# A hybrid decoder layer on one core: 24 of 32 activation tiles turned by VectorE and stored block by block, and three smaller edits in TensorE's and ScalarE's order

## The chip, the core and the metric

The kernel runs on one core of a Trainium2 chip. The metric is the device time of one execution in microseconds (us), given as the median of several runs. PE is TensorE, PEld its weight loads, DVE is VectorE, ACT is ScalarE, POOL is GpSimd, SP is SyncE, which here only issues DMAs; SPq is its queue. A line such as L825 is a line of the kernel before.

## What is computed

One layer of a decoder trunk over 2048 tokens of width 1024, all in float32. Cut to what matters:

```python
xn   = rms_norm(x, mix_norm_w)                       # 2048 x 1024
proj = xn @ w_in                                     # six groups of 512 columns: q, f, v, g, lru_x, lru_gate
mixed = concat(hgrn2(q, f, v, g), rglru(lru_x, lru_gate))   # chunkwise recurrences over the tokens
h    = x + mixed @ w_out
hn   = rms_norm(h, ffn_norm_w)                       # h * (mean(h^2) + eps)^-0.5 * ffn_norm_w
gate, up = split(hn @ w_gate_up)                     # 2 x 2816 columns
h    = h + (silu(gate) * up) @ w_down
out  = rms_norm(h, final_norm_w)
```

## The kernel before

**Stages.** The tokens go through in two halves of 1024, and each half in two pieces of 512 or eight tiles of 128 tokens. The order of the program is: half 0's mixers and output projection, half 1's mixers and output projection (the first loop `for half in range(2)`), then for half 0 the gate/up products (`ffn_up`) and the down products (`down_quads`), then the same for half 1. Every large product is three float32r matmuls of rounded parts (high by high, low by high, high by low), so one 128x512 block costs three passes per 128 rows of depth. The output projection, gate/up and down products take seven block products in place of eight (names p1 to p7; the banks `quad_a`, `quad_e`, `quad_f`, `quad_g` hold them in gate/up).

**What `h_steps` does (lines 1377 to 1404).** After the output projection, h lies in DRAM by tokens. The gate/up products need hn with features on the partitions. So for each of the 8 tiles of a half, `scale` loads the two 512-wide pages of the tile (n = 0 and 1, names `hs`), takes the sum of squares on ACT, the factor on DVE and POOL, and multiplies on DVE. `turn` then turns each page with `transposed` (lines 245 to 249): four 128x128 transposes on PE (L248, tiles `tp_hs`) into a PSUM bank of the tag `aux`, a copy to SBUF by ACT (L1398, tiles `hths` of the tag `late`, five buffers), and one store on SP's queue (L1399) into the DRAM tensor `hn`, whose rows are features. That makes 32 pages, 16 in each half.

**Where these steps stand.** Half 0's steps are the list `later` that is emptied in the next pass of the loop, one entry behind each of the eight `tok_mm` of half 1's first product (lines 1183 to 1188, tiles `pv`, 24 matmuls each). Half 1's steps run in half 0's `ffn_up`: the list has 14 empty entries and then 14 for each tile, one taken behind each of the seven products of a quad, so that one tile is scaled and turned in every two quads. Half 0's hn is read again in half 1's output projection, half 1's in half 0's `down_quads`; both are far behind the stores.

**Who sets the order.** The program is written in the order above, but a scheduler with its own simulated clock sets the order of instructions on each engine; each engine then runs its list in order and waits at semaphores. `tc.issue_after(ins)` puts what the block creates behind `ins`, for instructions of `ins`'s own engine. The buffers of a tag are given out in turn (`late` 5, `aux` 4 banks, `mm` 4 banks, the split weights `w` 9).

**The other places that the change touches.** `diagonals` and `over_rows` (lines 595 to 606) and `row_spread` (608 to 615) spread 512 row factors over all partitions: a diagonal matrix of the factors is multiplied by a matrix of ones, four float32 matmuls of 128x128. They are used three times besides the first piece of half 0: for the second piece of half 0 (L614) and for both pieces of half 1 (L605). In `ffn_up` the seven products of the first quad of a half are made in the order p1, p5, p6, p7, p2, p3, p4; p3 adds to the bank of p5 (`quad_e`), so its first matmul can't start before ACT has copied that bank out (L870). At the end of the last `down_quads`, `square` and `finish` normalise the last tiles: for each, the sum is squared on ACT (L980), the root taken on ACT (L993), its reciprocal on DVE (L994), then the rows are scaled on both engines and stored. The chains `behind("act", ...)` and `behind("dve", ...)` keep these in order. `root_table` (L998 to L1001) is to load ACT's table for the root early: it calls a bare table load inside `issue_after` of a matmul, with no data that it reads.

Of the kernel before, what the change touches and what calls it, by code (L numbers as in the profile page):

```python
# [9 lines left out]
F32R = mybir.dt.float32r  # L10
AF = mybir.ActivationFunctionType
ALU = mybir.AluOpType

P = 128
# [9 lines left out]
CW = 512  # L24
NC = T // CW
TPC = CW // P
NTT = T // P
SUB = 32
# [9 lines left out]
def hybrid_layer(ctx: ExitStack, tc: tile.TileContext, x, x_t, norm_w, cols, w_in, gate_w, w_out, w_gu, w_down, out):  # L38
    nc = tc.nc
    const = ctx.enter_context(tc.tile_pool(name="const", bufs=1))  # L40
# [5 lines left out]
    def f(t):  # L46
        return t.bitcast(F32)
# [17 lines left out]
    def late(nm):  # L65
        return sb.tile([P, CW], F32, tag="late", name=nm, bufs=5)
# [4 lines left out]
    def aux(nm):  # L71
        return psp.tile([P, CW], F32, tag="aux", name=nm)
# [27 lines left out]
    v = nc.vector  # L100
    ones = const.tile([P, 1], F32, name="ones")
    nc.gpsimd.memset(ones, 1.0)
    tinies = const.tile([P, 17, 4], F32, name="tinies")
    n4 = [0]

# [139 lines left out]
    def transposed(tt, n, src, nm):  # L245
        ps = aux("tp_%s_%d" % (nm, n))
        for j in range(4):
            nc.tensor.transpose(out=ps[:, j * P : (j + 1) * P], in_=src[:, j * P : (j + 1) * P], identity=ident)  # L248
        return ps.rearrange("p (k t) -> p k t", t=P)
# [343 lines left out]
        return xw  # L593

    def diagonals(c, rs, nm):
        dg = late("dg" + nm)
        for tt in range(TPC):
            v.tensor_scalar(out=dg[:, tt * P : (tt + 1) * P], in0=ident, scalar1=rs[:, tt : tt + 1], scalar2=None, op0=ALU.mult)
        return dg

    def over_rows(dg, nm):
        pbc = aux("tpb" + nm)
        for tt in range(TPC):
            ts = slice(tt * P, (tt + 1) * P)
            nc.tensor.matmul(pbc[:, ts], lhsT=ones.broadcast_to([P, P]), rhs=dg[:, ts], start=True, stop=True)  # L605
        return pbc

    def row_spread(c, rs, nm="x0"):
        nm = f"{nm}_{c}"
        pbc, dg = aux("tpb" + nm), late("dg" + nm)  # L610
        for tt in range(TPC):
            ts = slice(tt * P, (tt + 1) * P)
            v.tensor_scalar(out=dg[:, ts], in0=ident, scalar1=rs[:, tt : tt + 1], scalar2=None, op0=ALU.mult)
            nc.tensor.matmul(pbc[:, ts], lhsT=ones.broadcast_to([P, P]), rhs=dg[:, ts], start=True, stop=True)  # L614
        return pbc
# [170 lines left out]
    class Sums:  # L786
# [8 lines left out]
        def make(self, i):  # L795
# [21 lines left out]
            split([w[:, s, :] for s in range(2)], x)  # L817
            self.op[name] = w

    def product(ps, w, b, first):  # L820
        for k in range(4):
            ks = slice(k * P, (k + 1) * P)
            hi, lo = b[0][:, k, :], b[1][:, k, :]
            for n, (s, x) in enumerate(((0, hi), (1, hi), (0, lo))):
                ins = nc.tensor.matmul(  # L825
                    ps, lhsT=w[:, s, ks], rhs=x, start=first and k + n == 0, stop=k == 3 and n == 2, skip_group_check=not first
                )
        return ins.ins


# [15 lines left out]
    def ffn_up(half, bops, between=()):  # L846
        between = list(between)
        q0 = half * 2 * NPAIR
        for q in range(q0, q0 + 2 * NPAIR):
# [7 lines left out]
            for i, name in enumerate(ORDER):  # L857
                if q == q0 and i not in s.done:
                    s.make(i)
                if q == q0 and name == "p2":  # L860
                    with tc.issue_after(last):
                        last = product(dst[name], s.op.pop(name), bops[name], False)
                else:
                    last = product(dst[name], s.op.pop(name), bops[name], i < 4)
                if name == "p1":
                    e1 = page("e1" + nm)
                    nc.scalar.copy(out=e1, in_=b1)
# [129 lines left out]

    def root_table(matmul):  # L998
        with tc.issue_after(matmul.ins):
            ins = nc.scalar.preload_act_table(AF.Sqrt)  # L1000
        tail["act"] = ins.ins  # L1001

    def behind(eng, make):
# [72 lines left out]
    def down_quads(half, groups, hp, extra):  # L1076
# [18 lines left out]
        for s, (gr, i) in enumerate(seq):  # L1095
# [10 lines left out]
            for tt in range(TPC):  # L1106
                tsl = slice(tt * P, (tt + 1) * P)
                ps = banks[tt]
                for q in range(gr.n):
                    ahi, alo = (z[:, tsl] for z in a[q])  # L1110
                    whi, wlo = (w[z][:, q, :] for z in range(2))
                    for n, (x, y) in enumerate(((ahi, whi), (ahi, wlo), (alo, whi))):
                        ins = nc.tensor.matmul(  # L1113
                            ps, lhsT=x, rhs=y, start=first and q + n == 0, stop=q == gr.n - 1 and n == 2, skip_group_check=not first
                        )
                if half and end and name == "p5" and tt == 0:
                    root_table(ins)
                g = c * TPC + tt
                if half and end and name in ("p3", "p4"):
# [30 lines left out]
    for half in range(2):  # L1150
# [226 lines left out]
        def h_steps(g, half=half, ffn_row=ffn_row):  # L1377
            ps = []
            nm = f"hs{half}_{g}"

            def scale():
                if not ffn_row:
                    ffn_row.append(wvec(1, f"wffn{half}"))
                for n in range(2):
                    p = page(f"{nm}_{n}")
                    nc.sync.dma_start(out=p, in_=h_d[half][g][n])
                    ps.append(p)
                rs = rstd_of(ps, nm)
                for n in range(2):
                    v.scalar_tensor_tensor(  # L1390
                        out=ps[n], in0=ps[n], scalar=rs, in1=ffn_row[0][:, n * CW : (n + 1) * CW], op0=MUL, op1=MUL
                    )

            def turn():
                for n in range(2):
                    pt = transposed(g, n, ps[n], nm)
                    q = late(f"ht{nm}_{n}")
                    nc.scalar.copy(out=q.rearrange("p (k t) -> p k t", t=P), in_=pt)  # L1398
                    nc.sync.dma_start(  # L1399
                        out=hn_d[half][n][:, :, g * P : (g + 1) * P].rearrange("k p t -> p k t"),  # L1400
                        in_=q.rearrange("p (k t) -> p k t", t=P),
                    )

            return scale, turn

# [122 lines left out]
```

## Time and profile before

| | us |
|---|---|
| median of three runs | 2062.3 (2061.43 to 2062.76) |
| the profiled execution: device time | 2061.29 |
| the profiled execution: span of the trace | 2059.6 |

The profile is one execution. Its span goes from the first to the last instruction or transfer; 1.69 us of the device time lie around it. "busy" is the time in which an engine had an instruction in work. A wait is given with the engine, line and tile that ended it. A timeline row gives start, length, engine, line, operation, tiles, shapes and a count of merged instructions; the length of a merged PE row includes the tail of its last matmul, which overlaps the next row, so the pace is read from starts. The chain of work that ended last gives the start and length of each link.

### The profile page before, as it was taken

To read this page: it belongs to the slowest core of one execution; us is meant where nothing else is said; L and a number is where in the kernel's file an instruction comes from. 1 tells how busy PE (TensorE), PEld (TensorE's weight loads), DVE (VectorE), ACT (ScalarE), POOL (GpSimd) and SP (SyncE) were. 2 spreads that over 40 slices of the span, in tenths; PEclk is the share of its full clock that TensorE was granted. 3 is DMA by queue.
4 is the path that set the end of the run, shared out by engine and by line. 5 is a ranking of instruction groups with operands and counts; after the bars stand their busy time and mean duration, and the time that the engine had idled before them with its cause. 6 is when DMAs were issued, how large, how long until landed. Compare 5 with 4: busy or idle time off the path is not lost.

```text
span 2059.6 us, 26494 instructions
## 1 busy us (share of the span) xinstructions
PE 2050.5 (100%) x9532; PEld 1702.7 (83%) x9532; DVE 1557.8 (76%) x2581; ACT 1023.0 (50%) x1700; POOL 196.8 (10%) x339
## 2 busy tenths in 40 slices
PE   9999999999999999999999999999999999999998
PEld 8888888888888888888888888888888888888887
DVE  7878779836887699877777778879776676667766
ACT  8677765456776545343343344346433333344434
POOL 1001100000000000322222210001110010010000
PEclk9999999999999999999999999999999999999999
DMA  7234115831111365655555588665432232268642
GB/s 287 93 104 138 56 42 211 290 123 42 42 42 42 106 223 173 211 183 183 185 184 179 179 307 301 236 213 189 138 133 91 84 133 97 85 250 289 226 156 103
DMA packets 160228, 326.84 MB, mean 159 GB/s; under 512 B 14432, under 2 KB 31072, under 8 KB 160096
## 3 DMA queue, kind: packets, MB, share of 16 engines
q1 hardware_dynamic: 140448, 261.40, 37.4%
q0 software_dynamic: 19360, 63.45, 8.5%
q8 instruction: 75, 1.23, 0.3%
q14 instruction: 57, 0.47, 0.1%
q10 hardware_dynamic: 288, 0.29, 0.0%
HBM read 242.77 MB, written 82.31 MB: 158 GB/s over the span
## 4 chain that ended last, share of the span: by engine, by line
PE 95%; ACT 2%; DVE 1%; DMA 1%; issue 0%; POOL 0%; SPq 0%; DVEq 0%; ACTq 0%
PE quad_e L825 12%; PE quad_g L825 12%; PE quad_a L825 12%; PE pda L1113 11%; PE pdb L1113 8%; PE quad_f L825 6%; PE pox L1357 4%; PE poyp L1357 3%; PE pa L260 2%; PE pa L261 2%; PE pa L262 2%; PE pb L262 2%; PE pb L261 2%; PE pb L260 2%; PE pv L638 2%; PE pg L273 1%
## 5 line engine op out<-in xcount | busy, mean ns | idle before, releaser
L825 PE MATMUL quad_a<-act_a,wgu_a 128*128 128x512 f32 x528 | 132.3, 390 | 0.0
L825 PE MATMUL quad_e<-act_c,wgu_c 128*128 128x512 f32 x528 | 128.4, 389 | 0.5 <-ACT e L870 0.5
L825 PE MATMUL quad_e<-act_e,wgu_e 128*128 128x512 f32 x528 | 128.7, 389 | 0.0
L825 PE MATMUL quad_g<-act_g,wgu_g 128*128 128x512 f32 x528 | 127.6, 389 | 0.0
L825 PE MATMUL quad_f<-act_f,wgu_f 128*128 128x512 f32 x528 | 127.5, 389 | 0.0
L825 PE MATMUL quad_a<-act_b,wgu_b 128*128 128x512 f32 x528 | 127.1, 389 | 0.0
L825 PE MATMUL quad_g<-act_d,wgu_d 128*128 128x512 f32 x528 | 126.8, 389 | 0.0
L825 PEld LDWEIGHTS quad_e<-act_c,wgu_c 128*128 128x128 f32 x528 | 99.1, 188 | 21.4 <-ACT e L870 0.9
L825 PEld LDWEIGHTS quad_a<-act_b,wgu_b 128*128 128x128 f32 x528 | 99.1, 188 | 20.7
L825 PEld LDWEIGHTS quad_g<-act_g,wgu_g 128*128 128x128 f32 x528 | 99.1, 188 | 20.6
L825 PEld LDWEIGHTS quad_e<-act_e,wgu_e 128*128 128x128 f32 x528 | 99.1, 188 | 20.6
L825 PEld LDWEIGHTS quad_g<-act_d,wgu_d 128*128 128x128 f32 x528 | 99.1, 188 | 20.6
L825 PEld LDWEIGHTS quad_f<-act_f,wgu_f 128*128 128x128 f32 x528 | 99.1, 188 | 20.5
L825 PEld LDWEIGHTS quad_a<-act_a,wgu_a 128*128 128x128 f32 x528 | 98.5, 188 | 19.9
L681 DVE TENSOR_TENSOR u<-u,quad_g 128x512 f32<-128x512 f32 x88 | 60.2, 684 | 64.0 <-PE quad_g L825 64.0
L260 PE MATMUL pa<-xn,whi_in 128*128 128x512 f32 x256 | 101.5, 397 | 0.1
L262 PE MATMUL pb<-xn,whi_in 128*128 128x512 f32 x256 | 100.4, 392 | 0.0
L261 PE MATMUL pa<-xn,wlo_in 128*128 128x512 f32 x256 | 100.4, 392 | 0.0
L261 PE MATMUL pb<-xn,wlo_in 128*128 128x512 f32 x256 | 100.4, 392 | 0.0
L262 PE MATMUL pa<-xn,whi_in 128*128 128x512 f32 x256 | 100.4, 392 | 0.0
L260 PE MATMUL pb<-xn,whi_in 128*128 128x512 f32 x256 | 100.1, 391 | 0.0
L292 ACT ACT_TABLE_LOAD x69 | 88.5, 1283 | 2.4 <-PEq L1517 1.2
(373 smaller groups left out, 4971.5 us busy)
## 6 DMA issues: line engine op xcount, KB each, us to landing
raw<-in_w_gu SPq DMA_DIRECT2D x88, 512.0 KB, 4.1
raw_in<-in_w_in SPq DMA_DIRECT2D x47, 512.0 KB, 3.6
ao_p<-as POOLq DMA_DIRECT2D x88, 256.0 KB, 2.7
b<-hn SPq DMA_DIRECT2D x48, 256.0 KB, 3.9
wds<-in_w_down POOLq DMA_DIRECT2D x44, 256.0 KB, 4.4
wd_p<-wds POOLq DMA_DIRECT2D x44, 256.0 KB, 2.7
x<-in_x SPq DMA_DIRECT2D x32, 256.0 KB, 5.4
res<-in_x SPq DMA_DIRECT2D x32, 256.0 KB, 6.4
```

Of the source, the lines that this page charges most:

```text
L260: nc.tensor.matmul(ps, lhsT=whi[:, ks], rhs=hi, start=(k == 0), stop=False)
L261: nc.tensor.matmul(ps, lhsT=wlo[:, ks], rhs=hi, start=False, stop=False)
L262: nc.tensor.matmul(ps, lhsT=whi[:, ks], rhs=lo, start=False, stop=(k == KT - 1))
L273: nc.tensor.matmul(ps, lhsT=hi, rhs=wlo[:, ks], start=False, stop=False)
L292: in_line(lambda: nc.scalar.preload_act_table(func))
L638: ins = nc.tensor.matmul(banks[tt], lhsT=a, rhs=w, start=(k + i == 0), stop=(k == KT - 1 and i == 2))
L681: return (e or v).tensor_tensor(out=out, in0=a, in1=b, op=op)
L825: ins = nc.tensor.matmul(ps, lhsT=w[:, s, ks], rhs=x, start=first and k + n == 0, stop=k == 3 and n == 2, skip_group_check=not first)
L1113: ins = nc.tensor.matmul(ps, lhsT=x, rhs=y, start=first and q + n == 0, stop=q == gr.n - 1 and n == 2, skip_group_check=not first)
L1357: nc.tensor.matmul(ps, lhsT=x_, rhs=y_, start=first and q + m == 0, stop=q == 3 and m == 2, skip_group_check=not first)
```

## The change

- `turn` in `h_steps`: for both pages of half 1's tiles and for page n = 0 of half 0's, 24 pages of 32, the four PE transposes and ACT's copy are replaced by one DVE instruction (`v.transpose`, on chip a STREAM_TRANSPOSE) that turns each 32x32 block of the 128x512 page in place of the whole. The blocks are put in their places by the store: four DMAs of 32 partitions x 16 blocks x 32 elements, 64 KB each in runs of 128 bytes, where one DMA of 256 KB in runs of 512 bytes stood. The eight n = 1 pages of half 0 stay as they were.
- `diagonals` and `over_rows`: the factors are split into a rounded part and a rest, two float32r diagonals of 512 columns, and two 128x512 matmuls with a rounded matrix of ones add up in one bank. `row_spread` uses them for the second piece of half 0; its first piece stays as it was. On DVE there are eight instructions of 128x128 where there were four.
- First quad of a half in `ffn_up`: p3 is to come behind the middle of p7 on PE.
- `root_table`: instead of the bare load, a root of the first tile's running sum into a column that is overwritten later; it is called behind p7's first tile and no longer behind p5's.

```diff
     def diagonals(c, rs, nm):
-        dg = late("dg" + nm)
+        dg = [sb.tile([P, CW], F32R, tag="late", name=f"dg{s}{nm}", bufs=5) for s in range(2)]
         for tt in range(TPC):
-            v.tensor_scalar(out=dg[:, tt * P : (tt + 1) * P], in0=ident, scalar1=rs[:, tt : tt + 1], scalar2=None, op0=ALU.mult)
+            ts, r = slice(tt * P, (tt + 1) * P), rs[:, tt : tt + 1]
+            v.tensor_scalar(out=dg[0][:, ts], in0=ident, scalar1=r, scalar2=None, op0=ALU.mult)
+            v.scalar_tensor_tensor(out=dg[1][:, ts], in0=ident, scalar=r, in1=f(dg[0][:, ts]), op0=ALU.mult, op1=ALU.subtract)
...
-        for tt in range(TPC):
-            ts = slice(tt * P, (tt + 1) * P)
-            nc.tensor.matmul(pbc[:, ts], lhsT=ones.broadcast_to([P, P]), rhs=dg[:, ts], start=True, stop=True)
+        for s in range(2):
+            nc.tensor.matmul(pbc, lhsT=ones_r.broadcast_to([P, P]), rhs=dg[s], start=(s == 0), stop=(s == 1))
...
+                elif q == q0 and name == "p3":
+                    with tc.issue_after(mid):
+                        last = product(dst[name], s.op.pop(name), bops[name], False)
...
+                if q == q0 and name == "p7":
+                    mid = halfway["ins"]
...
     def root_table(matmul):
         with tc.issue_after(matmul.ins):
-            ins = nc.scalar.preload_act_table(AF.Sqrt)
+            ss = sums_f[1, 0]
+            ins = nc.scalar.activation(out=ss[:, 3:4], in_=ss[:, 2:3], func=AF.Sqrt)
...
                 for n in range(2):
-                    pt = transposed(g, n, ps[n], nm)
                     q = late(f"ht{nm}_{n}")
-                    nc.scalar.copy(out=q.rearrange("p (k t) -> p k t", t=P), in_=pt)
-                    nc.sync.dma_start(
-                        out=hn_d[half][n][:, :, g * P : (g + 1) * P].rearrange("k p t -> p k t"),
-                        in_=q.rearrange("p (k t) -> p k t", t=P),
-                    )
+                    if half or n == 0:
+                        v.transpose(out=q, in_=ps[n])
+                        to = hn_d[half][n].rearrange("k (u a) t -> a (k u) t", a=SUB)
+                        for i in range(TPC):
+                            t1 = g * P + i * SUB
+                            nc.sync.dma_start(
+                                out=to[:, :, t1 : t1 + SUB],
+                                in_=q[i * SUB : (i + 1) * SUB].rearrange("p (j b) -> p j b", b=SUB),
+                            )
+                    else:
...
```

Here is how three places move. In the rows of the changed kernel the line numbers are its own (L248 is L250 there, L825 is L832, L232 is L234, L980 is L994). The numbers at the end of a name are those of buffers.

PE in half 1's first product, behind its third tile of tokens (`pv_0_2`); `tp_hs_1_0` and `tp_hs_1_1` are the turned pages of half 0's tile 1. Before:

```order
L273 MATMUL pv_0_2_3847<-wlo_in_3_3690,xn_0_01_3388 128x512
L274 MATMUL pv_0_2_3847<-whi_in_3_3689,xn_0_11_3390 128x512
L248 MATMUL tp_hs_1_0_3886<-ident,hs_1_0_3818 128x128 x4
L248 MATMUL tp_hs_1_1_3894<-ident,hs_1_1_3820 128x128 x4
L272 MATMUL pv_0_3_3902<-whi_in_0_3671,xn_0_00_3387 128x512
L273 MATMUL pv_0_3_3902<-wlo_in_0_3672,xn_0_00_3387 128x512
```

and now:

```order
L275 MATMUL pv_0_2_3856<-wlo_in_3_3701,xn_0_01_3399 128x512
L276 MATMUL pv_0_2_3856<-whi_in_3_3700,xn_0_11_3401 128x512
L250 MATMUL tp_hs_1_1_3902<-ident,hs_1_1_3831 128x128 x4
L274 MATMUL pv_0_3_3909<-whi_in_0_3682,xn_0_00_3398 128x512
L275 MATMUL pv_0_3_3909<-wlo_in_0_3683,xn_0_00_3398 128x512
```

Four of the eight transposes between two tiles of tokens are gone; in half 0's `ffn_up` all eight between two quads are.

PE in the first quad of half 0's `ffn_up`: `quad_e_0_0<-act_c` is the first matmul of p3, `quad_f` is p6, `quad_g` p7, `quad_a_0_1` the next quad's p1. Before:

```order
L825 MATMUL quad_a_0_1_7360<-act_a_0_6789,wgu_a_0_1_7233 128x512
L825 MATMUL quad_e_0_0_7216<-act_c_0_7175,wgu_c_0_0_7205 128x512
L825 MATMUL quad_f_0_0_7217<-act_f_0_6982,wgu_f_0_0_7172 128x512 x2
L825 MATMUL quad_f_0_0_7217<-act_f_0_6983,wgu_f_0_0_7172 128x512
L825 MATMUL quad_f_0_0_7217<-act_f_0_6982,wgu_f_0_0_7172 128x512 x2
```

and now:

```order
L832 MATMUL quad_a_0_1_7355<-act_a_0_6784,wgu_a_0_1_7228 128x512
L832 MATMUL quad_f_0_0_7212<-act_f_0_6977,wgu_f_0_0_7167 128x512 x2
L832 MATMUL quad_f_0_0_7212<-act_f_0_6978,wgu_f_0_0_7167 128x512
L832 MATMUL quad_f_0_0_7212<-act_f_0_6977,wgu_f_0_0_7167 128x512 x2
L832 MATMUL quad_f_0_0_7212<-act_f_0_6978,wgu_f_0_0_7167 128x512
L832 MATMUL quad_g_0_0_7213<-act_g_0_6979,wgu_g_0_0_7182 128x512 x2
L832 MATMUL quad_g_0_0_7213<-act_g_0_6980,wgu_g_0_0_7182 128x512
L832 MATMUL quad_g_0_0_7213<-act_g_0_6979,wgu_g_0_0_7182 128x512 x2
L832 MATMUL quad_g_0_0_7213<-act_g_0_6980,wgu_g_0_0_7182 128x512
L832 MATMUL quad_e_0_0_7211<-act_c_0_7170,wgu_c_0_0_7200 128x512
```

p3's first matmul has moved behind twelve matmuls of p6 and p7.

ACT in the last group of the last `down_quads`: `jf` are squares of finished rows, `aop_g` the split operand of p7. Before, the table load of `root_table` is the fourth row of ACT's whole list (L1000, behind the load of the parameters), and another one stands ahead of the first root (L993). Here nothing stands between the third square and p7's operand:

```order
L980 ACTIVATE jf_1_0_16877,sf_1_16876<-hd_1_0_15689 128x512
L980 ACTIVATE jf_2_0_16900,sf_2_16899<-hd_2_0_15691 128x512
L232 CAST aop_g_1_8_17032<-ra_g_1_8_16954 128x1024
L232 CAST aop_g_1_8_17046<-ra_g_1_8_16956 128x512
L980 ACTIVATE jf_3_0_16919,sf_3_16918<-hd_3_0_15693 128x512
```

and now:

```order
L994 ACTIVATE jf_1_0_16840,sf_1_16839<-hd_1_0_15652 128x512
L994 ACTIVATE jf_2_0_16863,sf_2_16862<-hd_2_0_15654 128x512
L1015 ACT_TABLE_LOAD
L1015 ACTIVATE sf_0_16816<-sf_0_16816 128x1
L234 CAST aop_g_1_8_16994<-ra_g_1_8_16917 128x1024
L234 CAST aop_g_1_8_17008<-ra_g_1_8_16919 128x512
```

The load at the start of ACT's list and the load ahead of the first real root are both gone; one load and a root of one column stand ahead of p7's operand.

More of the change, by code (lines that the diff above doesn't have):

```diff
@@ L102, in hybrid_layer @@
     nc.gpsimd.memset(ones, 1.0)
+    ones_r = const.tile([P, 1], F32R, name="ones_r")
+    nc.gpsimd.tensor_copy(out=ones_r, in_=ones)
     tinies = const.tile([P, 17, 4], F32, name="tinies")
@@ L609, in row_spread @@
         nm = f"{nm}_{c}"
+        if c:
+            return over_rows(diagonals(c, rs, nm), nm)
         pbc, dg = aux("tpb" + nm), late("dg" + nm)
@@ L818, in make @@
             self.op[name] = w
+    halfway = {}
     def product(ps, w, b, first):
@@ L827, in product @@
                 )
+            if k == 1:
+                halfway["ins"] = ins.ins
         return ins.ins
@@ L1115, in down_quads @@
                         )
-                if half and end and name == "p5" and tt == 0:
+                if half and end and name == "p7" and tt == 0:
                     root_table(ins)
@@ L1395, in turn @@
                 for n in range(2):
-                    pt = transposed(g, n, ps[n], nm)
                     q = late(f"ht{nm}_{n}")
-                    nc.scalar.copy(out=q.rearrange("p (k t) -> p k t", t=P), in_=pt)
-                    nc.sync.dma_start(
-                        out=hn_d[half][n][:, :, g * P : (g + 1) * P].rearrange("k p t -> p k t"),
-                        in_=q.rearrange("p (k t) -> p k t", t=P),
-                    )
+                    if half or n == 0:
[8 more added lines that the diff above has]
+                    else:
+                        pt = transposed(g, n, ps[n], nm)
+                        nc.scalar.copy(out=q.rearrange("p (k t) -> p k t", t=P), in_=pt)
+                        nc.sync.dma_start(
+                            out=hn_d[half][n][:, :, g * P : (g + 1) * P].rearrange("k p t -> p k t"),
+                            in_=q.rearrange("p (k t) -> p k t", t=P),
+                        )
             return scale, turn
```

## The prediction, made before the changed kernel was run

> **What bounds the kernel.** I read the page first: busy shares and the chain that ended last.
>
> ```profile
> span 2059.6 us, 26494 instructions
> PE 2050.5 (100%) x9532; PEld 1702.7 (83%) x9532; DVE 1557.8 (76%) x2581; ACT 1023.0 (50%) x1700; POOL 196.8 (10%) x339
> PE 95%; ACT 2%; DVE 1%; DMA 1%; issue 0%; POOL 0%; SPq 0%; DVEq 0%; ACTq 0%
> ```
>
> PE is in work for 2050.5 of 2059.6 us. The waits of PE say the same: three in the whole program, 1.5 us.
>
> ```profile
> PE warm L543 <- PEq L1517: 0.8, 1, 0.8
> PE quad_e L825 <- ACT e L870: 0.5, 1, 0.5
> PE pr L468 <- DVE v L435: 0.2, 1, 0.2
> ```
>
> So a PE instruction that goes away is time gained one for one, as long as what replaces it doesn't make PE wait; work added on DVE, SP or the DMA engines costs nothing until then. The sum below prices PE's work by pace (start to start), not by the length of a row, since neighbouring rows overlap.
>
> **Part 1: transposes of half 1's 16 pages.** The chain of waits has one link of quad_g per quad. While tiles are turned, two quads take one period, and after the last turned tile one quad.
>
> ```profile
> 920.93 2.72 PE quad_g L825 x12
> ...
> 959.91 2.72 PE quad_g L825 x12
> ...
> 1173.64 2.72 PE quad_g L825 x12
> ...
> 1192.68 2.72 PE quad_g L825 x12
> ```
>
> The period with a turned tile is 959.91 - 920.93 = 38.98 us; two quads without are 2 x (1192.68 - 1173.64) = 38.08 us, which is 168 matmuls at 2.72/12 = 0.227 us. Eight transposes cost 0.90 us, and eight tiles 8 x 0.90 = 7.2 us.
>
> **Part 2: transposes of half 0's n = 0 pages.** The timeline of PE in half 1's first product has a group of eight behind every 24 matmuls; two groups are 412.03 to 418.37 = 6.34 us apart, and 24 x 0.227 = 5.44, so again 0.90 us for eight. Four stay. What a group of four small ones costs is seen at the old row factors, in half 0's output projection:
>
> ```profile
> 412.03 1.04 PE L248 MATMUL tp_hs<-ident,hs 128*128 128x128 f32 x8
> 418.37 1.03 PE L248 MATMUL tp_hs<-ident,hs 128*128 128x128 f32 x8
> 338.52 0.61 PE L605 MATMUL tpbx<-dgx,ones 128*128 128x128 f32 x4
> 339.20 0.40 PE L1357 MATMUL pox<-wlo_o_p,mx_f 128*128 128x512 f32 x1
> ```
>
> From 338.52 to 339.20 there are four small passes and one wide matmul: 0.68 - 0.227 = 0.45 us for four. So eight groups shrink by 0.90 - 0.45 = 0.45 us: 3.6 us.
>
> **Part 3: row factors.** One set of four float32 matmuls shows as eight passes:
>
> ```profile
> 50.40 1.05 PE L614 MATMUL tpbx<-dgx,ones 128*128 128x128 f32 x8
> 51.52 0.39 PE L261 MATMUL pa<-xn,wlo_in 128*128 128x512 f32 x1
> 46.70 0.87 DVE L613 TENSOR_SCALAR dgx<-ident,ss_x 128x128 f32<-128x128 f32 x4
> 289.25 1.65 DVE L598 TENSOR_SCALAR dgx<-ident,ss_x 128x128 f32<-128x128 f32 x8
> L414 DVE SCALAR_TENSOR_TENSOR S<-S,G,pu 128x128 f32<-128x128 f32 x32 | 11.0, 345 | 0.6
> ```
>
> 51.52 - 50.40 = 1.12 us with one wide matmul among them: 0.89 us a set. Two 128x512 float32r matmuls take 2 x 0.227 = 0.45 (the price of every other wide one here). Three sets: 3 x 0.44 = 1.3 us. DVE makes four more pieces a set; a scalar_tensor_tensor of 128x128 takes 0.345 us, 1.4 us a set. The first set's diagonals were done at 46.70 + 0.87 = 47.6 and PE takes them at 50.4, so 1.4 us of cover is left (without it, what is missing would be PE's wait); the other two sets' were made at 289 and are taken from 338.5 on.
>
> **Part 4: the early root.** The end of the timeline:
>
> ```profile
> 2027.56 8.32 PE L1113 MATMUL pda<-wd_g,aop_g 128*128 128x512 f32 x36
> 2039.81 1.28 ACT L993 ACT_TABLE_LOAD   x1
> 2042.25 0.62 ACT L980 ACTIVATE jf<-hd 128x512 f32<-128x512 f32 x1
> 2044.15 0.62 ACT L980 ACTIVATE jf<-hd 128x512 f32<-128x512 f32 x1
> 2043.88 8.32 PE L1113 MATMUL pda<-wd_d,aop_d 128*128 128x512 f32 x36
> 2052.80 0.16 DVE L994 RECIPROCAL sf<-sf 128x1 f32<-128x1 f32 x1 [0.48 <-ACT sf L993]
> 2052.88 0.67 DVE L681 TENSOR_TENSOR hd<-hd,pda 128x512 f32<-128x512 f32 x1
> ```
>
> ACT loads the table at 2039.81 with the tail's chain behind it. From there it takes a row of tiles every 1.90 us (2042.25 to 2044.15), PE delivers one every 9 x 0.227 = 2.04 us: ACT catches up only 0.14 us a row, and at the last row DVE is still held by the reciprocal of the row before (2052.80). PE's last matmul ends at 2043.88 + 8.32 = 2052.20 and DVE's addition follows at 2052.88. With the load's 1.28 us out of the chain ACT is ahead of PE by then, and the addition waits for PE alone: up to 0.68 us gained. The load now stands on ACT behind the squares of p2's tiles and ahead of p7's operand; between p2 and p7 PE has p6 and p5, 72 matmuls or 16.3 us, which hide it. The bare load at the program's start that also goes is worth nothing, as ACT then waited for the parameters:
>
> ```profile
> 4.30 0.51 ACT L575 ACTIVATE xw<-xk,par 128x256 fp32r<-128x256 f32 x1 [0.49 <-DMA par<-in_cols]
> ```
>
> **Part 5: p3 behind p7's middle.** PE's 0.45 us wait is here:
>
> ```profile
> 793.06 0.59 ACT L870 COPY e<-quad_e 128x512 f32<-128x512 f32 x1 [0.57 <-PE quad_e L825]
> 793.70 0.50 PE L825 MATMUL quad_e<-act_c,wgu_c 128*128 128x512 f32 x1 [0.45 <-ACT e L870]
> 801.51 0.68 DVE L233 TENSOR_TENSOR act_f<-b,act_f 128x512 fp32r<-128x512 f32 x1
> 802.91 0.39 PE L825 MATMUL quad_f<-act_f,wgu_f 128*128 128x512 f32 x1
> ```
>
> With twelve matmuls ahead of it (2.7 us) the copy is done in time. What is late next is p6's second half: its low operand is ready at 801.51 + 0.68 = 802.19, and PE would come for it at 802.91 - 0.45 = 802.46. It just holds: 0.45 us gained.
>
> **What is added.** DVE gets 24 turns, which no trace here shows. Nearest rows of 128x512:
>
> ```profile
> L306 DVE TENSOR_SCALAR sf<-sf,tinies 128x512 f32<-128x512 f32 x16 | 8.6, 537 | 22.4 <-ACT lg L294 22.4
> L380 DVE COPY kut<-pk 128x512 f32<-128x512 f32 x16 | 10.9, 682 | 0.1
> L492 DVE TENSOR_TENSOR_SCAN t<-r,hst,ig 128x512 f32<-128x512 f32 x16 | 20.4, 1277 | 0.3
> ```
>
> Between 0.54 and 1.28 us; I take the copy's 0.68, as a turn too reads and writes each element once. In half 1 two turns stand in DVE's list ahead of wgu_e of the next quad. In the period of 39 us DVE is busy 29.5:
>
> ```profile
> 411.00:417.00 6.00, 6.00 (x32) 5.04 (x31) 1.29 (x3) 2.79 (x7) 0.54 (x1) 1.00 0.32 96
> 405.00:411.00 6.00, 6.00 (x32) 5.06 (x31) 2.05 (x4) 2.79 (x7) 0.54 (x1) 1.00 1.01 361
> 920.00:959.00 39.00, 39.00 (x178) 32.39 (x177) 29.50 (x49) 15.22 (x28) 9.14 (x16) 1.00 0.53 182
> ```
>
> (stretch, its length, busy time of PE, PEld, DVE, ACT and POOL with counts, PE's clock, DMA share, GB/s). With 1.4 us more in 38.1 it is at 81%, with the scan's price at 84%. What the turns hold up has its own lead:
>
> ```profile
> 850.44 0.69 DVE L233 TENSOR_TENSOR wgu_e<-s,wgu_e 128x512 fp32r<-128x512 f32 x1 [0.76 <-ACT wgu_e L232]
> 865.23 1.75 PE L825 MATMUL quad_e<-act_e,wgu_e 128*128 128x512 f32 x7
> ```
>
> 865.23 - 851.13 = 14.1 us between the split and its first use, against 1.4 to 2.6 us. In half 0's stage DVE is busy 1.29 of 6 us. ACT loses 24 copies and gains slack.
>
> The stores go from 24 DMAs to 96, and from 512 runs of 512 bytes a page to 2048 of 128. On SP an issue takes 0.38 us (the store's row below): 72 more are 27 us, in half 0's stage 9 us of 47, behind which the weights for later products stand, in half 1 18 us of 305.
>
> ```profile
> L1399 SPq DMA_DIRECT2D hn<-hths x32: 359/380/1413, 407.0 to 1125.4; - x32
> ```
>
> On the DMA engines, in 411 to 417 little else than two stores (512 KB) ran: 0.32 x 16 engines x 6 us = 30.7 us for 576 KB, 27 ns for 512 bytes; wide loads (405 to 411) took 97 us for 2166 KB, 23 ns for 512 bytes. So a run of 128 bytes costs at least 23/4 = 6 ns and, if the count alone matters, 27 ns; above that the trace has no row. I take 27, the near row in kind. Then a page costs 2048 x 27 = 55 us over 16 engines, 3.5 us. In half 0 a step is 5.44 + 0.45 = 5.89 us (94 us of 16 engines): 55 + 14 for the other page is a share of 0.73. In half 1 two pages a period add 111 - 28 = 83 us to the 0.53 x 16 x 39 = 331: 414 of 610, a share of 0.68. Cost to PE: none.
>
> **Sum.** 7.2 + 3.6 + 1.3 + 0.68 + 0.45 = 13.2 us. The new orders will have some new waits, as the old had 0.7 us of them behind the start; I take 0.5 off: 12.7. The profiled execution took 2061.29, so 2048.6; the median of the runs lies 1.0 us higher: 2062.3 - 12.7 = **2049.6 us**.
>
> **Rival 1, slower: the short runs choke the DMA engines.** Half 0's stage decides. ACT's squares of later tiles reuse the `late` buffers that the stores hold, and ACT's copies that empty the four banks of `pv` stand behind these squares. PE can run three tiles ahead, 3 x 5.9 = 17.7 us, so the stores may fall behind by 2.2 us a tile: (5.9 + 2.2) x 16 - 14 = 116 us for 2048 runs. The point is 56 ns a run, twice the 512-byte run. At 80 ns a step takes (164 + 14)/16 = 11.1 us, and PE loses 8 x 5.2 - 17.7 = 24 us; half 1 with 331 - 28 + 328 = 631 of 610 us is 1.3 us a period over and hides it behind its lead. Time: 2049.6 + 24 = 2074. Against: nothing in the trace costs over 27 ns a run. Chance 0.06.
>
> The Trainium skill, "DMA: Bandwidth & Descriptors", Specifications, speaks against the change: below 512 bytes the DMA engine reads, modifies and writes, and full rate needs at least that much. No run here shows a store so small. If the read doubled the 27 ns, an estimate of 54 ns, half 0 would end 15 us behind, just inside PE's lead, and the sum would stand; only more than that gives the 2074.
>
> **Rival 2: part of the gain goes into waits for DVE.** If PE met the turns at the eight tiles of half 1 with nothing to spare, 8 x 1.4 = 11 us would come back, 2061; a third to two thirds of that is 2053 to 2057. For it: DVE is the second busiest engine and each new order is the scheduler's own guess at a turn's length. Against: the 14.1 us of lead. Chance 0.12, a third of it above 2058.
>
> **Rival 3: the small edits don't do what they say.** If the table load is moved again or p3's wait turns up at p6, 1.1 us less: 2050.7, chance 0.08.
>
> **Chances.** Forecast 0.74. About 0.2% (4 us) is what a measurement tells from no change: from 2058.2 down it is faster. Faster 0.74 + 0.08 + 0.07 of rival 2 = 0.89; same 0.05; slower 0.06. The range leaves out rival 1 and the worst of rival 2; below, it takes the full 13.2, a median 1 us lower and 2 us for gains of order that I don't see: 2046.5 to 2056.
>
> **What would show it.** Right: periods of 38.1 us in half 0's gate/up, steps of 5.9 us at `pv`, no PE wait at 793, no table load at the end, PE waits under 2 us. Wrong: PE waiting for ACT's `v` copies or SP's weights around 450 us (rival 1), or for wgu splits between 850 and 1130 (rival 2); a turn over 1.3 us, or stores landing later than 10 us.

## The result and the profile after

The changed kernel takes **2049.34 us** (median of 4 runs, 2048.66 to 2049.44) against 2061.88 (4 runs, 2061.43 to 2062.76) on the same chip: 12.5 us less, a ratio of 0.9939 with a 95% interval of 0.9927 to 0.9951. The forecast was 2049.6.

The profile of the changed kernel shows the same kind of program as before, PE in work for the whole span:

```profile
span 2047.3 us, 26368 instructions
...
PE 2037.5 (100%) x9418; PEld 1690.2 (83%) x9418; DVE 1571.5 (77%) x2617; ACT 1009.8 (49%) x1676; POOL 196.1 (10%) x340
...
q1 hardware_dynamic: 178464, 261.40, 38.8%
...
hn<-hths SPq DMA_DIRECT2D x96, 64.0 KB, 2.6
```

PE has 114 matmul records fewer and is busy 13.0 us less. (The last two rows are SP's queue, with packets, MB and its share of the DMA engines' time, and the block stores from the view of DMA issues, with KB each and the median us to landing.) Its waits, again three:

```profile
PE warm L545 <- PEq L1542: 0.8, 1, 0.8
PE pv L643 <- DVE whi_in L586: 0.8, 1, 0.8
PE pr L470 <- DVE v L437: 0.7, 1, 0.7
```

The 0.5 us for ACT's copy of `e` is gone. New is 0.8 us for DVE's `whi_in` in the program's first microseconds, and the wait at `pr` has grown from 0.2 to 0.7. There is none near 450 us and none between 850 and 1130, where the rivals would have shown. One loss there doesn't stand in this list, because a weight load waited and not a matmul. Behind the last turned tile SP issued the eight block stores of its two pages, and the next load of weights (`raw`) behind them at 1114.06. DVE waited for that load, its `u` came late, and PE's weight load stood 0.34 us for `u` (the timelines of SP, DVE and PEld):

```profile
1109.80 4.15 SPq L1417 DMA_DIRECT2D hn<-hths  x8
...
1118.69 0.69 DVE L686 TENSOR_TENSOR s<-raw,raw 128x512 f32<-128x512 f32 x1 [3.08 <-DMA raw<-in_w_gu]
...
1123.15 2.61 PEld L832 LDWEIGHTS quad_g<-act_d,wgu_d 128*128 128x128 f32 x12 [0.34 <-DVE u L686]
```

The table below shows its price: 416.40 us for gate/up of half 0, where six of the kernels (e4 to e9), all with half 1's turns and the new order of products, take 416.16.

To see where the time went, I cut both timelines at the same instructions: the first matmul of half 0's output projection, of half 1's first product, of half 0's gate/up and of half 0's down projection, then PE's last group and the last store's issue. Before:

```profile
316.13 0.48 PE L1357 MATMUL pox<-whi_o_p,mx_a 128*128 128x512 f32 x1
...
394.79 0.39 PE L272 MATMUL pv<-whi_in,xn 128*128 128x512 f32 x1
...
787.42 2.88 PE L825 MATMUL quad_a<-act_a,wgu_a 128*128 128x512 f32 x12
...
1211.56 0.39 PE L1113 MATMUL pda<-wd_a,aop_a 128*128 128x512 f32 x1
...
2055.64 0.39 ACTq L1023 DMA_DIRECT2D out_h<-hd  x1
```

and after, with DVE's last addition:

```profile
316.12 0.48 PE L1372 MATMUL pox<-whi_o_p,mx_a 128*128 128x512 f32 x1
...
393.88 0.39 PE L274 MATMUL pv<-whi_in,xn 128*128 128x512 f32 x1
...
783.07 2.88 PE L832 MATMUL quad_a<-act_a,wgu_a 128*128 128x512 f32 x12
...
1199.47 0.39 PE L1128 MATMUL pda<-wd_a,aop_a 128*128 128x512 f32 x1
...
2031.79 8.32 PE L1128 MATMUL pda<-wd_d,aop_d 128*128 128x512 f32 x36
...
2040.14 0.69 DVE L686 TENSOR_TENSOR hd<-hd,pda 128x512 f32<-128x512 f32 x1
...
2042.89 0.38 ACTq L1038 DMA_DIRECT2D out_h<-hd  x1
```

The differences of these starts give a table by stage, for the experiments too (us; each column is one difference, "end" is the device time of the profiled execution less the last issue; from 1211.56 to PE's last group, 2043.88, it is 832.32 us in every kernel):

| kernel | median | to 316 | output projection of half 0 | half 1 up to gate/up | gate/up of half 0 | PE's last group to last issue | end |
|---|---|---|---|---|---|---|---|
| before | 2061.88 | 316.13 | 78.66 | 392.63 | 424.14 | 11.76 | 5.65 |
| after | 2049.34 | 316.12 | 77.76 | 389.19 | 416.40 | 11.10 | 6.51 |
| gain | 12.54 | 0.01 | 0.90 | 3.44 | 7.74 | 0.66 | -0.86 |
| e1_turns | 2051.98 | 316.70 | 78.67 | 389.34 | 417.47 | 11.77 | 6.20 |
| e2_small | 2059.26 | 316.05 | 77.76 | 392.66 | 423.43 | 11.12 | 5.75 |
| e3_all32 | 2045.04 | 315.97 | 77.77 | 386.96 | 417.03 | 11.11 | 5.79 |
| e4_half1 | 2051.92 | 316.03 | 77.77 | 392.65 | 416.16 | 11.12 | 5.87 |
| e5_runs2 | 2048.09 | 315.95 | 77.76 | 389.19 | 416.16 | 11.11 | 5.75 |
| e6_turn3 | 2048.91 | 316.07 | 77.77 | 389.18 | 416.15 | 11.12 | 6.35 |
| e7_rows | 2050.28 | 316.75 | 78.64 | 389.21 | 416.16 | 11.12 | 6.17 |
| e8_root | 2049.73 | 316.28 | 77.77 | 389.19 | 416.16 | 11.76 | 6.48 |
| e9_pool | 2074.10 | 316.10 | 77.76 | 413.92 | 416.16 | 11.12 | 5.82 |
| e10_runs4 | 2113.17 | 315.46 | 77.77 | 397.65 | 472.32 | 11.11 | 5.80 |
| e11_order | 2050.04 | 316.33 | 77.77 | 389.19 | 416.92 | 11.11 | 6.47 |

The stage columns repeat to some 0.02 us where nothing in the stage was changed, but for the 0.24 us just named. The first column varies by up to 0.9 us among kernels with the same program there, and the last by as much; that, not the stages, is why two medians can differ by half a microsecond and more. One execution of e11_order took 2554.41 us at a granted clock of 0.75 and is left out of its median.

The two paces that carry parts 1 and 2 are read from starts. The chain of waits has one period of half 0's gate/up, with two turned pages in it, from 914.02 to 952.10, 38.08 us; the timeline of PE has a step of `pv` from 410.73 to 416.64, 5.91 us:

```profile
914.02 2.72 PE quad_g L832 x12
...
952.10 2.72 PE quad_g L832 x12
```

```profile
410.73 0.60 PE L250 MATMUL tp_hs<-ident,hs 128*128 128x128 f32 x4
...
416.64 0.60 PE L250 MATMUL tp_hs<-ident,hs 128*128 128x128 f32 x4
```

What no trace of before could show, the turn and its stores, stands in the view of the tile `hths` (ns as least, median, most):

```profile
L1417 SPq DMA_DIRECT2D hn<-hths x96: 302/500/2767, 400.5 to 1113.4; - x96
L1413 DVE STREAM_TRANSPOSE hths<-hs x24: 668/704/711, 398.2 to 1109.7; 128x512 f32<-128x512 f32 x24
```

A turn takes DVE 0.704 us, and a store's issue on SP 0.50 us, not 0.38.

What a run of 128 bytes costs the DMA engines follows from the shares of SP's queue q1 in the page, which was this before:

```profile
q1 hardware_dynamic: 140448, 261.40, 37.4%
```

The bytes are the same. In time of one engine it was 0.374 x 16 x 2059.6 = 12,325 us, now 0.388 x 16 x 2047.3 = 12,710: 385 us more, although 24 pages of 512 runs of 512 bytes are gone. Such a page is worth 14.7 us: two ran in a step of 6.34 us at a share of 0.29, 0.29 x 16 x 6.34 / 2. So 24 x 2048 runs would cost 385 + 24 x 14.7 = 738 us, 15 ns a run. That is a little too much, as the other packets of the queue took longer too. The trace lists every packet: the 49,152 of 128 bytes took 648.6 us together, **13 ns a run**, and the 16,384 of 512 bytes before took 28.5 ns each. A short run costs about half a 512-byte run, and not the same as one. The windows at `pv` (before, then after; the share of the DMA engines is the last but one) agree, with 0.46 x 16 x 5.91 - 14.7 = 29 us for 2048 runs, 14 ns:

```profile
423.00:435.00 12.00, 12.00 (x63) 10.09 (x62) 2.47 (x6) 5.59 (x14) 1.08 (x2) 1.00 0.29 87
```

```profile
423.00:435.00 12.00, 12.00 (x59) 9.97 (x58) 4.39 (x8) 4.81 (x13) 1.08 (x2) 1.00 0.46 90
...
914.00:952.00 38.00, 38.00 (x170) 31.46 (x169) 30.25 (x50) 14.14 (x26) 9.23 (x16) 1.00 0.64 186
```

The Trainium skill, "DMA: Bandwidth & Descriptors", Specifications, wants 512 bytes for full rate, since a smaller write is read, changed and written back. The rate did fall, from 512 bytes in 28.5 ns to 128 in 13; but the doubled run of the estimate, 54 ns, is not what is measured.

### The profile page after: what moved, and what is told of

Read it like the earlier page. It is cut to its first block, busy times and chain, and to the rows that moved or that the text cites. A ratio compares the mean times of both kernels' runs of the same rounds, so it can differ in the third digit from the quotient of the medians.

```text
span 2047.3 us, 26368 instructions
## 1 busy us (share of the span) xinstructions
PE 2037.5 (100%) x9418; PEld 1690.2 (83%) x9418; DVE 1571.5 (77%) x2617; ACT 1009.8 (49%) x1676; POOL 196.1 (10%) x340
## 4 chain that ended last, share of the span: by engine, by line
PE 96%; DVE 2%; ACT 1%; DMA 1%; issue 0%; POOL 0%; SPq 0%; DVEq 0%
PE quad_g L832 12%; PE pda L1128 12%; PE quad_a L832 12%; PE quad_e L832 12%; PE pdb L1128 9%; PE quad_f L832 6%; PE pox L1372 4%; PE poyp L1372 3%; PE pa L262 2%; PE pa L263 2%; PE pa L264 2%; PE pb L264 2%; PE pb L262 2%; PE pb L263 2%; PE pv L643 2%; PE pg L275 1%
## 5 line engine op out<-in xcount | busy, mean ns | idle before, releaser
L832 PE MATMUL quad_a<-act_a,wgu_a 128*128 128x512 f32 x528 | 128.8, 389 | 0.0
L832 PE MATMUL quad_g<-act_g,wgu_g 128*128 128x512 f32 x528 | 127.6, 389 | 0.0
L832 PE MATMUL quad_f<-act_f,wgu_f 128*128 128x512 f32 x528 | 127.5, 389 | 0.0
L832 PE MATMUL quad_e<-act_e,wgu_e 128*128 128x512 f32 x528 | 127.3, 389 | 0.0
L832 PE MATMUL quad_a<-act_b,wgu_b 128*128 128x512 f32 x528 | 127.0, 389 | 0.0
L832 PE MATMUL quad_e<-act_c,wgu_c 128*128 128x512 f32 x528 | 127.0, 389 | 0.0
L832 PE MATMUL quad_g<-act_d,wgu_d 128*128 128x512 f32 x528 | 127.0, 389 | 0.0
L832 PEld LDWEIGHTS quad_g<-act_d,wgu_d 128*128 128x128 f32 x528 | 99.0, 188 | 20.9 <-DVE u L686 0.3
L832 PEld LDWEIGHTS quad_a<-act_a,wgu_a 128*128 128x128 f32 x528 | 99.1, 188 | 20.6
L832 PEld LDWEIGHTS quad_e<-act_c,wgu_c 128*128 128x128 f32 x528 | 99.1, 188 | 20.6
L832 PEld LDWEIGHTS quad_e<-act_e,wgu_e 128*128 128x128 f32 x528 | 99.1, 188 | 20.6
L832 PEld LDWEIGHTS quad_a<-act_b,wgu_b 128*128 128x128 f32 x528 | 99.1, 188 | 20.6
L832 PEld LDWEIGHTS quad_g<-act_g,wgu_g 128*128 128x128 f32 x528 | 99.1, 188 | 20.6
L832 PEld LDWEIGHTS quad_f<-act_f,wgu_f 128*128 128x128 f32 x528 | 99.1, 188 | 20.6
```

Source lines behind the costliest of these rows:

```text
L832: ins = nc.tensor.matmul(ps, lhsT=w[:, s, ks], rhs=x, start=first and k + n == 0, stop=k == 3 and n == 2, skip_group_check=not first)
```

## The experiments

The theory: PE is the bound, and each edit gains exactly the PE work or the PE wait that it takes away. The rivals: a part of the gain comes from elsewhere or is lost to new waits; the short runs or the turns are close to taking over. Every kernel was timed against the kernel before on its own chip; the medians of before were 2061.78, 2062.12 and 2061.99 us.

### The parts alone

**e1_turns** is the kernel before with only `turn` exchanged:

```diff
-                    pt = transposed(g, n, ps[n], nm)
                     q = late(f"ht{nm}_{n}")
+                    if half or n == 0:
+                        v.transpose(out=q, in_=ps[n])
...
```

> The kernel before with the 24 turns and their block stores alone. Theory (PE is the bound, a PE instruction that goes is time gained): 7.2 us of half 1's pages and 3.6 us of half 0's, 10.8 us below the 2061.9 of the kernel before: 2051.1; a period of 38.1 us in half 0's gate/up, a step of 5.9 us at pv. Rival (the small edits were needed to place the turns, or carry more of the 12.5 us than their sum of 2.4): 2053 or more, with new PE waits between 400 and 1130 us.

2051.98 us, ratio 0.9951 (0.9938 to 0.9963): 9.8 us gained. Half 1 up to gate/up gains 3.29 us and gate/up 6.67; there the old wait at `quad_e` remains, and one for DVE's `u` appears behind the last turned tile, as in the changed kernel. (Here the chain of waits itself runs through the eight stores on SP, the load of `raw` and DVE's list.) Against the 416.16 us of other kernels gate/up lost 1.31 us: 0.76 at `quad_e` (see e11) and 0.55 at `u`. The theory holds for the two stages but for that wait; its 2051.1 was 0.9 too low. In the profiled execution the first column is 0.57 us longer than before and the end 0.55.

**e2_small** is the changed kernel with the old `turn`:

```diff
-                    if half or n == 0:
-                        v.transpose(out=q, in_=ps[n])
...
+                    pt = transposed(g, n, ps[n], nm)
```

> The changed kernel with every page turned by PE again: row factors, early root and product order alone. Theory as predicted: 1.3 + 0.68 + 0.45 = 2.4 us, 2059.5. Rival (after the trace of the changed kernel: the first set of row factors gains nothing, since PE waits for DVE's v at 164 us anyway, and the last store takes 0.45 us longer): 0.87 + 0.65 + 0.45 - 0.45 = 1.5 us, 2060.4; PE's wait at pr is then 0.7 us.

2059.26 us, ratio 0.9987 (0.9979 to 0.9996): 2.5 us gained, as the theory said. By stage it is 0.90 + 0.71 + 0.64, and 0.08 in the first column. The rival's loss at the last store isn't there. The turns and the small edits add up: 9.8 + 2.5 = 12.3 of 12.5 us.

**e4_half1** turns by DVE in half 1 only:

```diff
-                    if half or n == 0:
+                    if half:
```

> The changed kernel with the turns in half 1 only; half 0's pages are turned by PE. Theory: 8 x 0.45 = 3.6 us above the changed kernel: 2052.9, pv steps of 6.34 us. Rival (half 0's stores already hold something up, so that less than the 3.6 us was gained there): 2050 to 2051.

2051.92 us, ratio 0.9951 (0.9939 to 0.9964), 2.6 above the changed kernel. The stage of half 0's turns took 392.65 against 389.19, so the pages of half 0 are worth 3.46 us. The median lies between the two forecasts, and the stage decides for the theory: the missing 0.9 us lie outside it, in gate/up (0.24 shorter than in the changed kernel) and in the end (0.64 shorter). Nothing was held up in the stage itself.

**e7_rows** has the old float32 row factors, with the old bodies of `diagonals` and `over_rows`:

```diff
-        if c:
-            return over_rows(diagonals(c, rs, nm), nm)
```

> The changed kernel with the old float32 row factors. Theory as predicted: 3 x 0.44 = 1.3 us above: 2050.6. Rival (the first set's 0.44 us is lost at once, as DVE's chain to v sets the time at 164 us): 0.87 us above, 2050.2, and PE's wait at pr falls from 0.7 to 0.2 us.

2050.28 us, ratio 0.9942 (0.993 to 0.9955), 0.94 us above the changed kernel, but not in the way the rival told: the wait at `pr` stays at 0.7. The second and third set are worth 78.64 - 77.76 = 0.88 us. The first set's share is in the first column, where profiles with old factors (before, e1, e7) stand at 316.13, 316.70 and 316.75 and those with new ones between 315.46 and 316.33. PE's work did shrink: from the first matmul of that set (50.51 in e7, 50.22 in the changed kernel) to the output projection, less the wait at `pr`, PE took 265.59 us in e7 and 265.16 in the changed kernel, 0.43 less (and 0.34 less than the 265.50 of the kernel before). But that wait lies between 0.14 and 0.74 us in profiles with new factors and between 0.23 and 0.86 in those with old ones. How much of the 0.43 is kept stays open.

**e8_root** and **e11_order** undo one edit each:

```diff
-            ss = sums_f[1, 0]
-            ins = nc.scalar.activation(out=ss[:, 3:4], in_=ss[:, 2:3], func=AF.Sqrt)
+            ins = nc.scalar.preload_act_table(AF.Sqrt)
...
-                if half and end and name == "p7" and tt == 0:
+                if half and end and name == "p5" and tt == 0:
```

```diff
-                elif q == q0 and name == "p3":
-                    with tc.issue_after(mid):
-                        last = product(dst[name], s.op.pop(name), bops[name], False)
```

> The changed kernel with the old load of the root's table behind p5's first tile. Theory: DVE's last addition follows PE's last matmul by 0.68 us again, 2050.0, with a table load on ACT among the tail's squares. Rival (what is gained there is lost at the last store, which took 4.41 us from its issue to the end in place of 3.96): the last store is back at 3.96 us and the time is unchanged within 0.3 us, 2049.5.

2049.73 us, ratio 0.994 (0.9927 to 0.9952). The last issue follows PE's last group by 11.76 us again instead of 11.10: 0.66 us. The table load stands at 2027.64 among the tail's squares; in the changed kernel it is at 1998.77, well ahead of them (the timeline of e8, then of the changed kernel):

```profile
2027.64 1.28 ACT L1007 ACT_TABLE_LOAD   x1
```

```profile
1998.77 1.28 ACT L1015 ACT_TABLE_LOAD   x1
```

The rival falls: "end" is 6.48 here as well, so the slower last store of the changed kernel has nothing to do with the root.

> The changed kernel with p3 of the first quad ahead of p7 again, as before. Theory: PE's wait for ACT's copy of e is back: 0.45 us, 2049.8. Rival (the list's order would have changed anyway, or the wait moves elsewhere): 2049.3, no wait at quad_e.

2050.04 us, ratio 0.9942 (0.9929 to 0.9954). Gate/up takes 416.92 us against 416.40, or 416.16 in the kernels without the wait for `u`, which isn't there in e11 either: the order is worth 0.76 us. PE's wait is back where it was:

```profile
789.57 0.50 PE L832 MATMUL quad_e<-act_c,wgu_c 128*128 128x512 f32 x1 [0.45 <-ACT e L881]
```

The wait costs more than the 0.45 us of this row. In its timeline eight matmuls from 788.73 on take 2.56 us to the start of the ninth at 791.29, where eight at 0.227 take 1.82.

### How far the rivals were

**e6_turn3** makes every turn three times:

```diff
-                        v.transpose(out=q, in_=ps[n])
+                        for _ in range(3):
+                            v.transpose(out=q, in_=ps[n])
```

> The changed kernel with every turn made three times into the same tile, so that a turned page costs DVE 2.1 us in place of 0.70. Theory (the lead of 14 us of the weight splits covers it; DVE at 30.3 + 2.8 = 33.1 of 38.1 us): no change, 2049.3, within 1 us. Rival 2 (PE meets the turns with little to spare): up to 8 x 2.8 = 22 us lost in half 1, 2055 to 2072, PE waiting for wgu splits between 850 and 1130.

2048.91 us, ratio 0.9935 (0.9923 to 0.9948), no change, though DVE makes 72 turns:

```profile
L1414 DVE STREAM_TRANSPOSE hths<-hs x72: 669/705/714, 398.8 to 1113.9; 128x512 f32<-128x512 f32 x72
```

In a period of gate/up DVE is busy 32.77 of 38 us (third column of the windows), and PE, the first, all of them:

```profile
914.00:952.00 38.00, 38.00 (x169) 31.48 (x168) 32.77 (x55) 14.75 (x28) 9.12 (x16) 1.00 0.66 199
```

Rival 2 falls with room to spare: even 2.8 us more a period is covered.

**e5_runs2** and **e10_runs4** store each turned page once or three times more, 2048 runs of 128 bytes in one DMA each, into a scratch tensor:

```diff
+                        nc.sync.dma_start(out=jr_d[half][g][n][:, :, :SUB], in_=q.rearrange("p (j b) -> p j b", b=SUB))
```

> The changed kernel with every turned page stored twice: one more DMA of 2048 runs of 128 bytes a page, into a scratch tensor that nobody reads. Theory (a run takes 14.6 ns, as the DMA share at 423 to 435 us of the changed kernel gives: 0.46 x 16 x 5.91 us less 13.5 for the other page, over 2048): a tile needs 60 + 13.5 = 73 us of 16 engines, 4.6 us of the 5.9: no loss, 2049.3, PE waits under 3 us, DMA share at pv 0.8. Rival 1 at 27 ns: 124 / 16 = 7.8 us a tile, 15 us behind after eight tiles with 8.8 us of weights besides, against 17.7 us of lead: 6 us lost, 2055. Rival 1 at 56 ns and more: 15 us a tile, 50 us lost, 2100.

2048.09 us, ratio 0.9932 (0.9918 to 0.9945): nothing lost, 389.19 in the stage. (It is 1.25 us faster than the changed kernel, but not through the stores: 0.24 us of that is the wait for `u` and 0.76 the end.) At `pv` the DMA engines are now nearly full, a share of 0.96:

```profile
405.00:453.00 48.00, 48.00 (x228) 39.79 (x227) 20.07 (x31) 21.39 (x47) 3.24 (x6) 1.00 0.96 206
```

The trace lists 98,304 packets of 128 bytes that took 1297.7 us together, 13 ns a run again.

> The changed kernel with every turned page stored four times: three more DMAs of 2048 runs of 128 bytes a page, into scratch tensors that nobody reads. Theory (rival 1's mechanism exists, its point is about here: the run with pages stored twice shows a DMA share of 0.93 in half 0, 18.2 ns a run): a tile needs 4 x 2048 x 18.2 + 13.5 = 163 us of 16 engines, 10.2 us against 5.9; after eight tiles 34 us behind against 17.7 us of lead, 17 us lost, 2065 (2060 to 2075), PE waiting around 450 us. At 14.6 ns a run: 8.3 us a tile, 19 us behind and 8.8 us of weights: 2050 to 2058. Rival (nothing that PE needs hangs on these stores): 2049.

2113.17 us, ratio 1.0248 (1.0235 to 1.0261). Stores do hold PE up at last, but mostly not where rival 1 put it. Half 0's stage lost only 8.5 us (397.65 against 389.19), which fits the theory's figure for 14.6 ns a run, not the one for 18.2. Gate/up, where I had expected no loss, lost 55.9. There the chain of waits shows how:

```profile
1001.42 4.27 SPq L1423
...
1005.73 3.68 SPq L1423
...
1010.49 0.79 SPq L1402
...
1011.34 5.11 DMA hs<-h
...
1016.50 0.59 ACT e L881
...
1017.13 5.30 PE quad_a L832 x12
```

An issue of 2048 runs holds SP for 1.64 us in the median and up to 4.59; the DMA engines' share was 0.91 in the stretch from 1002 to 1010, and 0.72 over gate/up. What holds an issue so long isn't shown. The load of the next tile's `hs` (L1402) stands behind such issues on SP, ACT's square waits for it, and ACT's copy `e` stands behind the square. PE waits for that copy seven times, 27.0 us, and each wait costs more than its length. The timeline of PE at one of them:

```profile
927.39 5.49 PE L832 MATMUL quad_a<-act_b,wgu_b 128*128 128x512 f32 x12 [4.86 <-ACT e L881]
```

and the window behind it, with the granted clock third from the right:

```profile
927.00:930.00 3.00, 2.61 (x6) 2.14 (x7) 3.00 (x6) 2.05 (x6) 1.97 (x4) 0.50 0.46 175
```

After 4.86 us without work the clock is 0.50, and twelve matmuls take 5.49 us, where a row of twelve takes 2.88 otherwise.

### A version further on

**e3_all32** turns half 0's n = 1 pages by DVE as well:

```diff
-                    if half or n == 0:
+                    if True:
```

> The changed kernel with half 0's n = 1 pages turned by DVE too, so that no tile is turned by PE. Theory (the DMA engines and SP carry it): eight times four transposes, 8 x 0.45 = 3.6 us less than the changed kernel's 2049.3: 2045.7, a pv step of 5.44 us. Rival (short runs choke the DMA engines or SP's queue at 16 stores a tile pair): at 27 ns a run a tile needs 4096 x 27 ns / 16 = 6.9 us against 5.44, with 8.8 us of weights behind; 8 x 6.9 + 8.8 = 64 against 43.5 + 16.3 us of PE's lead: some 4 us lost, 2050, and PE waits around 450 us.

2045.04 us, ratio 0.9921 (0.9907 to 0.9935), 16.7 us below the kernel before. All five runs, 2044.51 to 2048.27, lie below the four of the changed kernel. The theory's 2045.7 holds for the median; in the profiled execution (2046.95) the stage gained only 389.19 - 386.96 = 2.2 of 3.6 us, and gate/up lost 0.87 us to 416.16, nearly all at the same wait for `u` behind the last turned tile. SP's rows in the timeline show what is late there, and the wait of ACT that comes of it:

```profile
410.96 34.63 SPq L1417 DMA_DIRECT2D hn<-hths  x56
445.63 8.41 SPq L165 DMA_DIRECT2D raw_in<-in_w_in  x5
```

```profile
ACT whi_in L171 <- DMA raw_in<-in_w_in: 13.6, 4, 11.5
```

56 stores are issued back to back, 34.63 / 56 = 0.62 us each, and five loads of weights come behind them. SP issues without a pause here while the DMA engines' share is 0.79 (411 to 446 us): its queue is full before they are.

**e9_pool** gives the stores of half 0's n = 1 pages to POOL's queue:

```diff
-                            nc.sync.dma_start(
+                            (nc.gpsimd if half == 0 and n else nc.sync).dma_start(
```

> No tile turned by PE, and half 0's n = 1 pages stored through POOL's queue in place of SP's. Theory (with all pages turned SP's queue is the limit in half 0: 56 stores there took 34.63 us back to back, 0.62 us each, the weights' loads stood behind them and ACT waited 13.6 us for them; four issues a tile less give them way): ACT's wait for the weights below 6 us, 2045.0 or up to 1 us less, with a smaller spread than the 2044.5 to 2048.3 seen. Rival (the DMA engines, busy 0.79 of the stage, hold the buffers): DVE still waits some 10 us for earlier stores, and the time stays at 2045 with the same spread.

2074.10 us, ratio 1.006 (1.0048 to 1.0072): slower than the kernel before. Neither theory had it. POOL issues a store every 2.6 us, 0.66 of work and 1.9 ahead of it in which it waits for nothing that the profile shows, four to a tile, as its timeline shows:

```profile
415.81 0.57 POOL L229 TENSOR_TENSOR ss_hs<-ss_hs,tinies 128x1 f32<-128x1 f32 x1
...
420.23 0.66 POOL L1417 DMA_DIRECT2D hn<-hths  x1 [1.89 <-issue]
422.86 0.65 POOL L1417 DMA_DIRECT2D hn<-hths  x1 [1.97 <-issue]
...
426.05 0.57 POOL L229 TENSOR_TENSOR ss_hs<-ss_hs,tinies 128x1 f32<-128x1 f32 x1
```

POOL also makes a piece of each tile's row factor (L229), and that stands behind the stores. So a tile takes 10.2 us, 415.81 to 426.05 from factor to factor, DVE waits for that factor, its list falls behind, and PE waits for `wlo_in` at 461. The waits of the two (us, times, longest):

```profile
DVE hs L1405 <- POOL ss_hs L229: 47.3, 6, 10.2
...
PE pa L263 <- DVE wlo_in L172: 21.3, 1, 21.3
```

Whether the stores could go to a queue that is neither SP's nor POOL's wasn't tried.

## Why the prediction was right

**Parts 1 and 2** came as worked out. The period is 38.08 us as predicted, 8 x 0.90 = 7.2 us. (The chain has two links of `quad_g` a quad and not one, but the period was read rightly.) The step at `pv` is 5.91 against 5.89, so the stage gained 3.44 us (3.46 by e4) where 3.6 was said. **Part 5** had the right wait and too low a price, 0.76 us by e11 and 0.71 by e2 against 0.45: the prediction took the idle time of one row where the starts around it show the whole loss. With the 7.2 it makes 7.96 of the 7.98 us that gate/up gains in e4 to e9 without the wait for `u`; the changed kernel's 7.74 is 0.24 less for that wait. **Part 4**: 0.66 us by e8 and the table against "up to 0.68"; in the changed kernel DVE's addition follows PE's last group at once (2031.79 + 8.32 = 2040.11, 2040.14).

**Part 3** was right for two sets, 0.90 us for 0.88. For the first set PE's work shrank by 0.34 to 0.43 us where 0.44 was said. That it is gained one for one is not shown: PE meets DVE's chain at `pr` afterwards, and that wait differs by 0.6 us between profiles of the same program.

**New waits**: 0.5 us was taken off. The waits at `pv` and `pr` grew by 0.8 + 0.5 = 1.3 us, and the first column, in which both lie, is 316.12 as against 316.13, though 0.4 us of PE's work is gone from it; the wait for `u` cost 0.24. By medians 12.5 us came of 12.7. The profiled execution shows 11.9, since its end took 0.86 us longer; that column is between 5.65 and 6.51 in all kernels. So the mechanism is shown, but that the median came within 0.3 us of the forecast is in part luck: part 5 gained 0.3 us more than said, part 2 0.16 less and the first set perhaps nothing, and the end moves by more than that by itself.

**The price of the turn** (0.68, measured 0.704) was right, and e6 shows that it didn't matter. **The price of a run** was the term mis-sized: 27 ns were taken, with 6 as the lower end, and it is 13. Taking the run's count for the whole cost was the step that failed. The shares were lower for it, 0.46 for the predicted 0.73 at `pv` where only the page stores ran, 0.64 for 0.68 in half 1. The trace of before held a nearer row than the one taken: its list of packets has 128 of 212 bytes, 19 ns each in the mean. And that nothing in it costs over 27 ns a run holds for short runs alone; the 103,424 packets of 2048 bytes took 95 ns each.

**Rival 1** asked for 56 ns a run, and 13 was found. In total time, twice the runs cost nothing and four times cost 64 us. But the prediction looked at the DMA engines' share and at half 0. SP's queue, at 0.50 to 0.62 us an issue instead of the 0.38 taken, was full first in e3, its eight stores stand ahead of the late weights in the changed kernel's 0.24 us, and under the fourfold load most was lost beside gate/up, where half 1's pages are turned. **Rival 2** fell at three times its price. **Rival 3** fell: e8 and e11 show that the early root and the order each gain at least what was said, but for 0.02 us. None of PE's waits in the changed kernel is over 0.8 us, and the 96 block stores landed 2.6 us after their issue in the median.

## What to carry to other kernels

When PE is busy for the whole span, price its work by the start-to-start pace in the stage and sum what goes; here that gave 12.7 for 12.5 us. For the work that moves off PE ask which in-order queue it joins and what stands behind it there: in e3 and e9 SP's issues and POOL's time for a store became the limit, before the DMA engines or DVE did. Price a wait, too, by starts: the 0.45 us of one row cost 0.76. Cut two timelines at the same instructions and compare stage by stage; terms of half a microsecond then show which medians can't.

## What was not expected of the hardware

- A store's run of 128 bytes took 13 ns of a DMA engine where a 512-byte run took 28.5: a quarter of the bytes for half the time.
- The same kind of block store costs POOL 2.6 us and SP 0.50 to 0.62 us an issue; one issue with 2048 runs held SP for up to 4.59 us in e10, where the DMA engines' share was 0.91 around it.
- After 4.86 us and after 21.27 us of waiting the granted clock was 0.50. The Trainium skill, "TensorE: Matmul & The Clock Gate", Part 1, says that an idle window of about 3.4 us halves the clock until as long a busy one has passed. These rows agree as to the halving; the way back took longer, as the clock was still at 0.50 from 465 to 466, 4 us into the work, and at 1.00 from 467 on. After 1.97 us at 471 the matmuls kept their 0.40 us, where those after the long wait were still at 0.63 us more than 4 us on:

```profile
461.42 0.79 PE L263 MATMUL pa<-xn,wlo_in 128*128 128x512 f32 x1 [21.27 <-DVE wlo_in L172]
...
465.85 0.63 PE L264 MATMUL pa<-xn,whi_in 128*128 128x512 f32 x1
...
471.43 0.51 PE L263 MATMUL pb<-xn,wlo_in 128*128 128x512 f32 x1 [1.97 <-DVE wlo_in L172]
471.77 0.40 PE L264 MATMUL pb<-xn,whi_in 128*128 128x512 f32 x1
```

```profile
461.00:464.00 3.00, 2.58 (x6) 2.11 (x7) 0.36 (x1) 0.00 (x0) 0.66 (x1) 0.50 0.87 146
```
